# Layer 0's mixer reads x a second time in feature-major form, in place of transposing it on chip

## The chip, the cores and the metric

The kernel runs on one core of a Trainium2 chip. The metric is the device time in microseconds of one execution. The engines are TensorE (PE, with its weight loads as PEld), VectorE (DVE), ScalarE (ACT), GpSimd (POOL) and SyncE (SP), which issues the loads and stores. Each engine works through its own queue strictly in the order in which the program has it, and waits for the others by semaphores.

## The reference

Two residual layers over x of 1024 tokens by 1024 features in float32. Layer 0's mixer begins with an RMS norm and one input projection, whose columns go to a gated MLP (u, v) and to attention with eight heads (q, k, v):

```python
def rms_norm(x, g):
    xf = x.astype(jnp.float32)
    return xf * lax.rsqrt(jnp.mean(xf * xf, -1, keepdims=True) + EPS) * g.astype(jnp.float32)

def even_mixer(h, w_in, ...):
    z = h @ w_in
    u, v, q, k, vb = jnp.split(z, [...], axis=-1)
    ...
    qh = rms_norm(heads(q), q_g)
    kh = rms_norm(heads(k), k_g)
    vh = heads(vb).astype(jnp.float32)
    ...

for layer in range(DEPTH):
    h = rms_norm(x, norm_mix_g[layer]).astype(x.dtype)
    mix = even_mixer(...) if layer % 2 == 0 else gla_mixer(...)
    x = x + mix.astype(x.dtype)
    h = rms_norm(x, norm_ffn_g[layer]).astype(x.dtype)
    x = x + conv_ffn(h, ...)
```

The rest (attention with a band of 128 and two dilated branches, gated linear attention in layer 1, the convolutional MLPs) is not touched by the change.

## The kernel before

Every matrix product runs on operands split in two fp32r parts, a high part (a cast) and a remainder (source minus high part); `split` makes them, `PASSES` multiplies high by high, high by low and low by high. The norm of layer 0 is not applied to x: its gain g0 is folded into the weights (`load_qkv` with `scaled`), and the inverse root mean square of each token, `r0[:, n]`, is applied where a product is evacuated.

`even` prepares x. It loops over the eight token tiles n of 128 rows. Each is loaded as 128 tokens by 1024 features (three buffers, tag "x"), PE transposes its eight 128x128 blocks into PSUM (`pt`), and ACT and DVE split them into `hq`, the feature-major operand of the projections; `hq[g][h]` holds the features of parity g of tile half h. ACT then squares the tile with a running sum, and POOL makes `r0[:, n]` of it (`inv_rms`, two short operations). After tile 1 the weights of head pair 0 are loaded and split.

`attention` runs four head pairs. `project(p)` loops over the eight token tiles: 24 matmuls of 128x384 into an accumulator `pj` (two PSUM banks), and then, for each tile: ACT squares q and k (`qn`, needs r0), DVE sums, POOL makes the inverse norm (`rq`), DVE scales `qn` from the accumulator, and ACT evacuates v (`vN`). The accumulator is free for the tile after next when both have read it. POOL and DVE split q and k (`qs`, `ks`), PE transposes them (`tq`, `tk`), ACT casts `qT`, ACT or DVE `kT`. `unit` does one tile's banded attention: scores (`sc`), masked minimum on DVE and exponential on ACT (`sm`), transposes (`pP`), a copy (`pT`) and the product with v (`po`). `dilated(p)` and the projection of pair p + 1 follow.

The program text is not the final order: a scheduler with a cost model of its own reorders each engine's queue when the kernel is built. Loads go out on one SP queue with eight semaphores in rotation, so that each load's issue waits for the landing of the load eight places ahead of it.

## Time and profile before

| what | value |
|---|---|
| time, three runs | 2174.93, 2177.8 (median), 2179.95 us |
| profiled execution | 2178.69 us, span 2176.9 us |
| granted TensorE clock, mean | 0.998 |
| instructions | 29864 |
| PE, PEld busy | 98%, 83% |
| DVE, ACT, POOL busy | 70%, 48%, 23% |
| HBM read, written | 239.02 MB, 108.59 MB |

The span runs from the first to the last instruction of the profiled execution; what lies around it is 1.8 us. A row of the timeline gives the start, the duration, the engine, the line, the operation and its operands, and in brackets how long the engine had been idle before it and what ended that. A row by stretches gives the busy time of each engine with its number of instructions, the granted clock, the share of the DMA engines and the GB/s. A row by groups gives the count, the busy time, the mean of one in ns and the idle time before the group.

### The profile page before, as it was taken

Reading aid. Unit: us, or ns where it says so; the run is one execution under the profiler, and the core shown is the slowest. Engines: PE = TensorE matmul, PEld = TensorE weight load, DVE = VectorE, ACT = ScalarE, POOL = GpSimd, SP = SyncE. Lnnn points to the kernel's source line nnn. Section 1 sums busy time; section 2 is a strip of 40 time slices with the busy share of each in tenths; the row PEclk is TensorE's granted clock in tenths of the full one; section 3 lists DMA queues with packets and bytes.
Section 4 is the critical chain, followed back from the end, with each engine's and each line's share of the span. In section 5 each row is a group of like instructions: output and inputs, shape, how many; then the busy total and the mean of one; then the engine's idle time right before and its main releaser. Section 6 shows DMA issues by size and latency. Waiting matters only on the chain.

```text
span 2176.9 us, 29864 instructions
## 1 busy us (share of the span) xinstructions
PE 2139.8 (98%) x10508; PEld 1812.1 (83%) x10508; DVE 1534.4 (70%) x2451; ACT 1034.1 (48%) x1998; POOL 490.8 (23%) x519
## 2 busy tenths in 40 slices
PE   8999999999999999999999999999999999999999
PEld 7999988877888888878889888878788888888887
DVE  6566655567887988755576777667788878885554
ACT  6455545355444444444454455534544444444443
POOL 4444421013342434100020011100333424320000
PEclk9999999999999999999999999999999999999999
DMA  4122212655544444675564233386544444557555
GB/s 158 48 81 63 78 55 77 212 204 201 158 156 160 160 165 160 197 268 198 194 210 129 71 97 97 117 268 242 201 160 153 153 156 159 165 179 277 201 195 202
DMA packets 157254, 349.59 MB, mean 161 GB/s; under 512 B 17408, under 2 KB 54272, under 8 KB 156720
## 3 DMA queue, kind: packets, MB, share of 16 engines
q1 hardware_dynamic: 157104, 347.68, 47.6%
q8 instruction: 83, 1.36, 0.3%
q14 instruction: 67, 0.55, 0.1%
HBM read 239.02 MB, written 108.59 MB: 160 GB/s over the span
## 4 chain that ended last, share of the span: by engine, by line
PE 87%; DMA 5%; DVE 3%; ACT 3%; issue 1%; POOL 0%; SPq 0%; DVEq 0%; ACTq 0%; POOLq 0%
PE puB L290 11%; PE pgB L290 11%; PE pv L190 6%; PE pj L190 6%; PE pgC L290 5%; PE puC L290 5%; PE pdB L397 5%; PE pdC L397 5%; PE pdO L397 4%; PE po L190 3%; PE puA L290 3%; PE pgA L290 3%; PE pdQ L397 2%; PE pdP L397 2%; PE pu L190 2%; PE pBq L992 2%
## 5 line engine op out<-in xcount | busy, mean ns | idle before, releaser
L101 DVE TENSOR_TENSOR da<-ar,da 128x512 fp32r<-128x512 f32 x154 | 106.3, 690 | 157.3 <-ACT da L100 157.2
L100 ACT CAST da<-ar 128x512 fp32r<-128x512 f32 x154 | 95.9, 623 | 211.1 <-PE pdC L397 91.6
L190 PE MATMUL po<-wo,hq 128*128 128x512 f32 x768 | 184.4, 395 | 1.6 <-ACT hq L100 1.0
L190 PEld LDWEIGHTS po<-wo,hq 128*128 128x128 f32 x768 | 141.6, 188 | 31.7 <-ACT hq L100 1.4
L190 PE MATMUL pv<-wv,hq 128*128 128x512 f32 (+2 forms) x768 | 139.8, 339 | 2.1 <-DVE b L1024 1.6
L397 PE MATMUL pdB<-dw,da 128*128 128x512 f32 x528 | 136.2, 391 | 1.0 <-ACT dw L100 1.0
L397 PE MATMUL pdC<-dw,da 128*128 128x512 f32 x528 | 135.8, 390 | 0.0
L190 PEld LDWEIGHTS pv<-wv,hq 128*128 128x128 f32 x768 | 119.0, 189 | 17.4 <-DVE b L1024 2.1
L397 PEld LDWEIGHTS pdB<-dw,da 128*128 128x128 f32 x528 | 98.6, 188 | 22.3 <-ACT dw L100 1.4
L190 PE MATMUL pj<-wq,hq 128*128 128x384 f32 x576 | 116.2, 343 | 0.2 <-ACT vN L720 0.2
L397 PEld LDWEIGHTS pdC<-dw,da 128*128 128x128 f32 x528 | 99.1, 188 | 20.5
L256 POOL TENSOR_TENSOR S1g<-rg 128x512 f32<-128x512 f32 x20 | 29.4, 1470 | 382.6 <-DMA wsd<-D 235.0
L140 POOL TENSOR_SCALAR rn<-ssq 128x1 f32<-128x1 f32 x24 | 10.6, 441 | 465.0 <-ACT h L148 245.4
L101 DVE TENSOR_TENSOR dw<-wr,dw 128x512 fp32r<-128x512 f32 x154 | 105.8, 687 | 9.5 <-ACT dw L100 9.1
L397 PE MATMUL pdO<-dw,da 128*128 128x512 f32 x396 | 102.2, 389 | 0.2 <-DVE dw L101 0.2
L100 ACT CAST dw<-wr 128x512 fp32r<-128x512 f32 x154 | 95.0, 617 | 13.0 <-DMA wr<-in_w_dn 7.5
L190 PEld LDWEIGHTS pj<-wq,hq 128*128 128x128 f32 x576 | 99.2, 189 | 0.5 <-ACT vN L720 0.4
L397 PEld LDWEIGHTS pdO<-dw,da 128*128 128x128 f32 x396 | 74.2, 188 | 16.0 <-DVE dw L101 0.6
L319 DVE SCALAR_TENSOR_TENSOR t<-g,cw,t 128x1022 f32<-128x1022 f32 x44 | 75.6, 1719 | 0.1
L303 DVE TENSOR_TENSOR g<-g,s1g 128x512 f32<-128x512 f32 x22 | 17.2, 783 | 77.1 <-ACT s1g L302 77.0
L318 DVE SCALAR_TENSOR_TENSOR t<-g,cw,t 128x1023 f32<-128x1023 f32 x44 | 59.4, 1351 | 16.7 <-ACT t L317 16.7
L320 ACT ACTIVATE t<-t 128x1024 f32<-128x1024 f32 x44 | 46.7, 1061 | 30.7 <-DVE t L319 30.6
(1073 smaller groups left out, 5465.8 us busy)
## 6 DMA issues: line engine op xcount, KB each, us to landing
ar<-actd SPq DMA_DIRECT2D x70, 512.0 KB, 3.5
rd<-in_w_down SPq DMA_DIRECT2D x44, 512.0 KB, 3.7
wsd<-D SPq DMA_DIRECT2D x88, 256.0 KB, 2.5
rg<-in_w_gate SPq DMA_DIRECT2D x42, 512.0 KB, 3.6
ru<-in_w_up SPq DMA_DIRECT2D x42, 512.0 KB, 4.6
wr<-wsd SPq DMA_DIRECT2D x40, 512.0 KB, 4.2
actd<-t SPq DMA_DIRECT2D x66, 256.0 KB, 2.2
wr<-in_w_dn SPq DMA_DIRECT2D x30, 512.0 KB, 4.9
```

The lines of the kernel that those rows point to most:

```text
L100: (hi or A.copy)(dst[0], src)
L101: (lo or V.tensor_sub)(dst[1], src, f32(dst[0]))
L140: G.tensor_scalar(r, ssq, 1.0 / n, EPS, op0=ALU.mult, op1=ALU.add)
L190: T.matmul(o, L[i], R[jj][:, sl], start=(k == 0 and (ii, jj) == PASSES[0]), stop=(k == nk - 1 and (ii, jj) == PASSES[-1]))
L256: G.tensor_tensor(sums[name], x, y, op=op)
L290: T.matmul(o, L[ii][:, j * P : j * P + P], right[p][:, jj, j, :], skip_group_check=more, start=(not more and j == 0 and (ii, jj) == PASSES ...
L303: V.tensor_add(C22, C22, s1)
L318: V.scalar_tensor_tensor(t[:, 1:], g[:, : S - 1], w(1), t[:, 1:], op0=ALU.mult, op1=ALU.add)
L319: V.scalar_tensor_tensor(t[:, 2:], g[:, : S - 2], w(0), t[:, 2:], op0=ALU.mult, op1=ALU.add)
L320: A.activation(t, t, AF.Silu)
L397: T.matmul(o, L[ii][:, t * P : t * P + P], R[jj], skip_group_check=more, start=start and not more and (ii, jj) == PASSES[0], stop=stop and ...
L992: T.matmul(o, L[ii][:, j * P : j * P + P], right[p][:, jj, j, :], skip_group_check=more, start=(not more and j == 0 and (ii, jj) == PASSES ...
```

## The change

The host hands x over a second time as `x_T`: for each token tile the features on the partitions, ordered by parity g, by j and then by token (feature k * 128 + c with k = 2j + g), so that one tile is one 512 KB load and needs no transpose. ACT casts the high part of parity 0, POOL that of parity 1, DVE makes both remainders from SBUF. The token-major x is still loaded, for the squares alone, which are now made in place. The eight transposes per tile and their PSUM tiles are gone.

Every tile has a place: feature tiles 0 to 3 and token tiles 0 to 3 share six buffers, feature tiles 4 and 5 have two, feature tiles 6 and 7 stand in the room that `qR` of pair 1 takes later (`xq`), token tiles 4 to 7 in that of `kT` of pair 1 (`xk`). The squares of token tiles 4 to 7 are written inside the first projection, ahead of its tiles 0 to 3 (`rest`, called as `early`). The weights of pair 0 and the q and k gains are loaded after the first feature tile, ahead of all others; `gains` is the first five lines of `attention`, moved.

```diff
             with tc.tile_pool(name="nrm", bufs=1, reuse_waits="tile") as pool:
+                Q.dma_start(g0, a["norm_mix_gT"])
+                xk = pq.tile([P, 4, S], F32, tag="kT", bufs=1, name="xk")
+                xq = pq.tile([P, 2, S], F32, tag="qR", bufs=1, name="xq")
+
+                def home(name, tag, bufs):
+                    return pool.tile([P, D], F32, tag=tag, bufs=bufs, name=name)
+
+                def statistics(n, xt):
+                    ssq = small.tile([P, 1], F32, tag="ssq", name=f"ssq{n}")
+                    A.activation(xt, xt, AF.Square, accum_out=ssq)
+                    inv_rms(ssq, 1, D, f"rn{n}", r0[:, n : n + 1])
+
+                def token_rows(n):
+                    xt = home(f"x0{n}", "a", 6) if n < 4 else xk[:, n - 4]
+                    Q.dma_start(xt, rows(a["x"], n))
+                    if n < 4:
+                        statistics(n, xt)
+
                 for n in range(NT):
-                    xt = pool.tile([P, D], F32, tag="x", bufs=3, name=f"x0{n}")
-                    Q.dma_start(xt, rows(a["x"], n))
+                    xt = home(f"xf{n}", "a", 6) if n < 4 else home(f"xf{n}", "b", 2) if n < 6 else xq[:, n - 6]
+                    xf = xt.rearrange("p (g j t) -> p g j t", g=2, j=4)
+                    Q.dma_start(xf, a["x_T"][n])
+                    for g in range(2):
+                        split(place(hq[g][n // 4], n), xf[:, g], hi=G.tensor_copy if g else None)
                     if n == 0:
-                        Q.dma_start(g0, a["norm_mix_gT"])
-                    for g in range(2):
-                        pt = ps.tile([P, 4, P], F32, tag="pt", name=f"pt{n}{g}")
-                        for j in range(4):
-                            k = 2 * j + g
-                            T.transpose(pt[:, j, :], xt[:, k * P : (k + 1) * P], ident)
-                        split(place(hq[g][n // 4], n), pt)
-                    if n == 1:
                         wq0 = load_qkv(0, wx)
-                    h = pool.tile([P, D], F32, tag="h", bufs=2, name=f"h{n}")
-                    ssq = small.tile([P, 1], F32, tag="ssq", name=f"ssq{n}")
-                    A.activation(h, xt, AF.Square, accum_out=ssq)
-                    inv_rms(ssq, 1, D, f"rn{n}", r0[:, n : n + 1])
+                        gqk = gains(pq)
+                        token_rows(0)
+                    elif n > 1:
+                        token_rows(n - 1)
+                token_rows(NT - 1)
+
+            def rest(n):
+                if n < 4:
+                    statistics(n + 4, xk[:, n])
...
-        def project(p, ws=None, then=None):
+        def project(p, ws=None, then=None, early=None):
...
             for n in range(NT):
+                if early:
+                    early(n)
                 pj = ps.tile([P, 512], F32, tag="pj", name=f"pj{p}{n}")
...
-        made = project(0, wq0)
+        made = project(0, wq0, early=rest)
...
         "x": A["x"][0],
+        "x_T": A["x"][0].reshape(NT, P, 4, 2, P).transpose(0, 4, 3, 2, 1),
```

What this makes of the queues is seen at three places. The first is the SP queue before, from the third x tile on; `x` with its number is a token tile (tiles 2 to 4 here), `wq1` are weights of pair 1, `hg` and `gT` small tables of later stages.

```order
L523 DMA x_399<-in_x 128x1024
L647 DMA gqk<-in_q_g 128x64 [waits DMAHW0_49]
L648 DMA gqk<-in_k_g 128x64 [waits DMAHW1_49]
L523 DMA x_420<-in_x 128x1024 [waits DMAHW2_49,PE_49,Activation_49]
L647 DMA gqk<-in_q_g 128x64 [waits DMAHW3_49]
L648 DMA gqk<-in_k_g 128x64 [waits DMAHW4_49]
L1129 DMA hg<-in_head_g 128x2 [waits DMAHW5_49]
L460 DMA gT_5177<-in_norm_ffn_gT 128x8 [waits DMAHW6_49]
L110 DMA wq10r<-in_w_qkv 128x768 [waits DMAHW7_49,DVE_49]
L523 DMA x_441<-in_x 128x1024 [waits DMAHW0_49,PE_49]
L110 DMA wq11r<-in_w_qkv 128x768 [waits DMAHW1_49,DVE_49]
```

After, at the same depth of the queue (g0, feature tile 0, the four weight loads, four `gqk`, token tile 0 and feature tiles 1 and 2 stand ahead). `xf` and `xq` are feature tiles (3 to 7 here), `x_389`, `x_401` and `x_413` are token tiles 1, 2 and 3, `xk` token tiles 4 to 7.

```order
L535 DMA x_389<-in_x 128x1024 [waits DMAHW5_49]
L542 DMA xf_395<-in_x_T 128x1024 [waits DMAHW6_49]
L535 DMA x_401<-in_x 128x1024 [waits DMAHW7_49,DVE_49,Activation_49]
L542 DMA xf_407<-in_x_T 128x1024 [waits DMAHW0_49]
L542 DMA xf_419<-in_x_T 128x1024 [waits DMAHW1_49]
L535 DMA xk<-in_x 128x1024 [waits DMAHW2_49]
L542 DMA xq<-in_x_T 128x1024 [waits DMAHW3_49]
L535 DMA xk<-in_x 128x1024 [waits DMAHW4_49]
L542 DMA xq<-in_x_T 128x1024 [waits DMAHW5_49]
L535 DMA xk<-in_x 128x1024 [waits DMAHW6_49]
L535 DMA x_413<-in_x 128x1024 [waits DMAHW7_49,Activation_49]
L535 DMA xk<-in_x 128x1024 [waits DMAHW0_49]
```

All sixteen tiles of x now stand ahead of the weights of pair 1, and token tile 3 stands behind token tiles 4, 5 and 6.

The second place is ACT around the evacuations `vN` of tiles 0 and 1 (`vN_575` and `vN_651`) before; `x_441` to `x_483` are token tiles 4 to 6.

```order
L536 ACTIVATE h_457,ssq_458<-x_441 128x1024 [waits DMAHW0_49,Activation_49,Pool_49]
L712 ACTIVATE qn_566<-pj_541,r_84 128x256 [waits PE_49,Pool_49]
L105 ACTIVATE wq_0_1363<-wq11r,g_83 128x384 [waits DMAHW1_49]
L105 ACTIVATE wq_1_1366<-wq11r,g_83 128x384 [waits DVE_49]
L100 COPY hq_85<-pt_422 128x4x128 [waits PE_49]
L712 ACTIVATE qn_642<-pj_617,r_84 128x256 [waits PE_49,Pool_49]
L100 COPY hq_87<-pt_429 128x4x128 [waits PE_49]
L720 ACTIVATE vN_575<-pj_541,r_84 128x128 [waits DVE_49]
L536 ACTIVATE h_478,ssq_479<-x_462 128x1024 [waits DMAHW4_49,Activation_49]
L100 COPY hq_86<-pt_443 128x4x128 [waits PE_49]
L720 ACTIVATE vN_651<-pj_617,r_84 128x128 [waits DVE_49]
L536 ACTIVATE h_499,ssq_500<-x_483 128x1024 [waits DMAHW7_49,Activation_49,Pool_49]
```

After, from behind `vN` of tile 0 and the cast of feature tile 4 on: `vN_567` is that of tile 1, `x_413` is token tile 3, the three `xk` are token tiles 4 to 6, `hq_86` the casts of feature tiles 5 to 7.

```order
L737 ACTIVATE qn_558<-pj_533,r_84 128x256 [waits PE_49,Pool_49]
L100 COPY hq_86<-xf_419 128x4x128 [waits DMAHW1_49]
L100 COPY hq_86<-xq 128x4x128 [waits DMAHW3_49]
L758 COPY qT_499<-tq_496 128x256 [waits PE_49]
L737 ACTIVATE qn_640<-pj_615,r_84 128x256 [waits DVE_49,Pool_49]
L764 COPY kT_447<-tk_502 128x16x32 [waits PE_49]
L100 COPY hq_86<-xq 128x4x128 [waits DMAHW5_49]
L530 ACTIVATE x_413,ssq_415<-x_413 128x1024 [waits DMAHW7_49,Activation_49]
L530 ACTIVATE xk,ssq_449<-xk 128x1024 [waits DMAHW2_49]
L530 ACTIVATE xk,ssq_529<-xk 128x1024 [waits DMAHW4_49,Activation_49]
L530 ACTIVATE xk,ssq_611<-xk 128x1024 [waits DMAHW6_49,Activation_49]
L745 ACTIVATE vN_567<-pj_533,r_84 128x128 [waits DVE_49]
```

Before, one square stood between the two evacuations; after, the squares of four token tiles do, with `qT` and `kT` of tile 0 and the casts of four feature tiles.

The third place is PE ahead of the projection of tile 3 (`pj_773`) before; `pt` are transposes of x tiles 4 and 5.

```order
L190 MATMUL pj_695<-wq_1_383,hq_87 128x384 x3
L190 MATMUL pj_695<-wq_0_388,hq_85 128x384 x3
L530 MATMUL pt_450<-ident,x_441 128x128 [waits DVE_49]
L530 MATMUL pt_450<-ident,x_441 128x128 x3
L730 MATMUL tq_584<-identr,qs_578 128x128 [waits DVE_49]
L730 MATMUL tq_584<-identr,qs_578 128x128
L190 MATMUL pj_695<-wq_1_391,hq_87 128x384 x3
L530 MATMUL pt_464<-ident,x_462 128x128 [waits DMAHW4_49,DVE_49]
L530 MATMUL pt_464<-ident,x_462 128x128 x3
L190 MATMUL pj_773<-wx_364,hq_85 128x384 [waits Activation_49]
L190 MATMUL pj_773<-wx_364,hq_85 128x384 x2
```

After, the projection of tile 3 is `pj_697`, and `tq`, `tk` and `sc0n` are tile 0's.

```order
L190 MATMUL pj_615<-wq_0_359,hq_85 128x384 x3
L190 MATMUL pj_615<-wq_1_362,hq_87 128x384 x3
L755 MATMUL tq_496<-identr,qs_490 128x128 [waits DVE_49]
L755 MATMUL tq_496<-identr,qs_490 128x128
L763 MATMUL tk_502<-identr,ks_491 128x128 [waits Activation_49,Pool_49]
L763 MATMUL tk_502<-identr,ks_491 128x128 [waits DVE_49]
L763 MATMUL tk_502<-identr,ks_491 128x128 x2
L684 MATMUL sc0n_511<-kT_447,qT_499 128x128 [waits Activation_49]
L684 MATMUL sc0n_511<-kT_447,qT_499 128x128
L684 MATMUL sc0n_518<-kT_447,qT_499 128x128 x2
L190 MATMUL pj_697<-wx_335,hq_85 128x384 [waits Activation_49]
```

The transposes of x are gone from between the matmuls, and the transposes and scores of tile 0 now stand ahead of the projection of tile 3.

More of the change, by code (lines that the diff above doesn't have):

```diff
@@ L538, in even, with gains @@
+                token_rows(NT - 1)
+            def rest(n):
+                if n < 4:
+                    statistics(n + 4, xk[:, n])
             with tc.tile_pool(name="at", bufs=2, reuse_waits="tile") as at, \
                     tc.tile_pool(name="av", bufs=1, reuse_waits="tile") as av:
-                return attention(ps, at, av, pq, pq0, par0, wx, wq0, masks, gm_open)
+                return attention(ps, at, av, pq, pq0, par0, wx, wq0, gqk, masks, rest, gm_open)
+    def gains(pq):
+        gqk = pq.tile([P, 2, 2, 64], F32, name="gqk", bufs=1)
+        for s in range(2):
+            Q.dma_start(gqk[:, 0, s, :], a["q_g"].partition_broadcast(P))
+            Q.dma_start(gqk[:, 1, s, :], a["k_g"].partition_broadcast(P))
+        V.tensor_scalar(gqk[:, 0], gqk[:, 0], -0.125, None, op0=ALU.mult)
+        gqk = gqk.rearrange("p a s c -> p (a s c)")
+        return gqk
@@ L641, in u_proj, with attention @@
         proj512(ps, load_half(a["w_vu"][1], "wu", g0), "pu", consume)
-    def attention(ps, at, av, pq, pq0, par0, wx, wq0, masks, gm_open):
-        gqk = pq.tile([P, 2, 2, 64], F32, name="gqk", bufs=1)
-        for s in range(2):
-            Q.dma_start(gqk[:, 0, s, :], a["q_g"].partition_broadcast(P))
-            Q.dma_start(gqk[:, 1, s, :], a["k_g"].partition_broadcast(P))
-        V.tensor_scalar(gqk[:, 0], gqk[:, 0], -0.125, None, op0=ALU.mult)
-        gqk = gqk.rearrange("p a s c -> p (a s c)")
+    def attention(ps, at, av, pq, pq0, par0, wx, wq0, gqk, masks, rest, gm_open):
         mband, mboth = masks
```

## The prediction

> **What bounds the kernel now.** I read the page first, then busy time by stretches of the start, then the engines' timeline there.

> ```profile
> PE 2139.8 (98%) x10508; PEld 1812.1 (83%) x10508; DVE 1534.4 (70%) x2451; ACT 1034.1 (48%) x1998; POOL 490.8 (23%) x519
> PE   8999999999999999999999999999999999999999
> ```

> TensorE (PE) is busy for 2139.8 of 2176.9 us, and only the first fortieth of the span, 54.4 us, shows less than nine tenths. The change touches just that fortieth. Behind it, what arrives late there stays late, so I ask at what time the PE queue reaches the same point of its program before and after. Busy time by stretch:

> ```profile
> core 0: us, PE busy (x) PEld busy (x) DVE busy (x) ACT busy (x) POOL busy (x), PEclk, DMA share, GB/s
> 0.00:10.00 10.00, 4.49 (x18) 3.65 (x19) 6.23 (x17) 6.59 (x12) 3.06 (x13) 1.00 0.82 277
> 10.00:20.00 10.00, 10.00 (x52) 9.93 (x52) 5.96 (x12) 7.28 (x16) 1.49 (x4) 1.00 0.74 272
> 20.00:30.00 10.00, 6.60 (x31) 6.29 (x30) 6.46 (x14) 7.15 (x16) 7.43 (x15) 0.70 0.67 240
> 30.00:40.00 10.00, 10.00 (x66) 9.86 (x65) 4.05 (x9) 5.08 (x11) 4.79 (x10) 0.96 0.19 61
> 40.00:50.00 10.00, 8.46 (x63) 7.75 (x62) 7.64 (x22) 5.58 (x16) 5.61 (x10) 1.00 0.01 2
> 50.00:60.00 10.00, 9.86 (x73) 9.43 (x72) 3.89 (x12) 4.67 (x14) 2.13 (x5) 1.00 0.13 37
> ```

> PE loses 5.5 us in the first stretch, 3.4 in the third and 1.5 in the fifth. In the third the granted clock falls to 0.70 on average. The timeline and two short stretches show how:

> ```profile
> 21.15 0.60 PE L530 MATMUL pt<-ident,x 128*128 128x128 f32 x4
> 25.15 1.12 PE L530 MATMUL pt<-ident,x 128*128 128x128 f32 x4 [3.40 <-DVE hq L101]
> 25.92 4.19 PE L190 MATMUL pj<-wx,hq 128*128 128x384 f32 x12
> 128.73 4.24 PE L190 MATMUL pj<-wq,hq 128*128 128x384 f32 x23
> 23.00:24.00 1.00, 0.00 (x0) 0.00 (x0) 0.10 (x1) 0.76 (x2) 0.98 (x1) 0.96 0.63 247
> 30.00:31.00 1.00, 1.00 (x6) 1.00 (x5) 0.00 (x1) 0.00 (x0) 0.14 (x1) 0.62 0.00 0
> ```

> PE stops at 21.75. The clock halves at about 23.9 (0.96 over that microsecond) and is whole again at about 30.8 (0.62), 5.6 us after work resumed. In between a 128x384 matmul takes 0.335 to 0.35 us; at full clock it takes 0.18 (23 in 4.24). This price returns below.

> **The change part by part. What it removes.** The 64 transposes of x go, with what PE waited for them:

> ```profile
> L530 PE MATMUL pt<-ident,x 128*128 128x128 f32 x64 | 11.9, 322 | 8.7 <-DMA x<-in_x 4.7 <-DVE hq L101 4.0
> L100 ACT CAST hq<-pt 128x512 fp32r<-128x512 f32 x16 | 9.3, 582 | 7.2 <-PE pt L530 7.1
> L101 DVE TENSOR_TENSOR hq<-pt,hq 128x512 fp32r<-128x512 f32 x16 | 11.0, 685 | 11.4 <-ACT hq L100 11.4
> L100 POOL CAST ks<-qn 128x256 fp32r<-128x256 f32 x13 | 5.6, 429 | 0.3 <-PE tk L738 0.3
> ```

> PE is relieved of 11.9 us of busy time. ScalarE (ACT) keeps 8 of its 16 casts, so it gives up 4.7 us. GpSimd (POOL) takes the other 8; no row has its 128x512 cast, but at twice the 0.43 us of the 128x256 one it is at most 0.86, about 7 us in all, on an engine that is busy for 12 of the first 30 us. VectorE (DVE) does the same 16 subtractions, now from SBUF. If PE were what sets the end of this stage, some 10 us would be won.

> **What it adds: eight more loads of 512 KB ahead of everything else.** What a load costs in the queue:

> ```profile
> 0.79 0.39 SPq L523 DMA_DIRECT2D x<-in_x  x1
> 4.61 1.06 ACT L536 ACTIVATE h<-x 128x1024 f32<-128x1024 f32 x1 [2.55 <-DMA x<-in_x]
> 7.83 0.33 SPq L647 DMA_DIRECT2D gqk<-in_q_g  x1
> 8.79 0.33 SPq L648 DMA_DIRECT2D gqk<-in_k_g  x1
> 9.76 0.33 SPq L1129 DMA_DIRECT2D hg<-in_head_g  x1
> 10.74 0.33 SPq L460 DMA_DIRECT2D gT<-in_norm_ffn_gT  x1
> 12.07 0.33 SPq L110 DMA_DIRECT2D wq10r<-in_w_qkv  x1
> 14.85 1.06 ACT L536 ACTIVATE h<-x 128x1024 f32<-128x1024 f32 x1 [0.78 <-DMA x<-in_x]
> ```

> From the ninth load on, each issue waits for the load eight places ahead of it. So 7.83, 8.79, 9.76 and 10.74 are the landings of the four 384 KB weight loads of pair 0, and 12.07 is that of x tile 2. That is 0.97 us per 384 KB and 1.3 per 512 KB. The next 512 KB tile landed at 14.85, 2.8 us later, with two of the small broadcast loads of gqk between: 0.73 us for each of those.

> In the changed SP order I add these up. The gain vector g0 goes first, so the feature-major tile 0 lands at 4.61 + 0.44 = 5.05. The weights follow with one tile less ahead of them, 7.83 - 1.3 = 6.5, 7.5, 8.5 and 9.4. Four gqk loads at 0.73 make 12.3. Then come fourteen 512 KB tiles up to and including token tile 3, which stands behind token tiles 4, 5 and 6: 12.3 + 14 x 1.31 = 30.6. Before, the same token tile landed at 14.85. With eight loads in flight the issue itself never runs dry. The gqk price could be nothing if small loads overlap; then token tile 3 lands at 27.7.

> **The wait that this makes.** The ACT queue is in program order, and in it the evacuation of v of tile 1 (vN, "vN1") now stands behind the square of token tile 3 and those of tiles 4, 5 and 6. The projection's accumulator has two banks, so projection tile 3 ("pj3") cannot start before vN1. Prices:

> ```profile
> L536 ACT ACTIVATE h<-x 128x1024 f32<-128x1024 f32 x8 | 8.4, 1055 | 5.2 <-DMA x<-in_x 5.2
> L536 ACT ACTIVATION_READ_ACCUMULATOR h<-x 128x1 f32 x8 | 1.5, 189 | 0.0
> 28.38 0.37 ACT L720 ACTIVATE vN<-pj,r 128x128 f32<-128x128 f32 x1 [1.49 <-DVE qn L716]
> 33.38 2.33 PE L190 MATMUL pj<-wx,hq 128*128 128x384 f32 x12
> 46.30 0.33 PE L730 MATMUL tq<-identr,qs 128*128 128x128 f32 x2 [0.85 <-DVE kT L739]
> 53.32 2.31 PE L190 MATMUL pj<-wx,hq 128*128 128x384 f32 x12
> 70.33 0.50 PE L738 MATMUL tk<-identr,ks 128*128 128x128 f32 x4 [0.62 <-ACT qT L733]
> 71.74 1.10 PE L689 MATMUL po0n<-vN,pT0n 128*128 128x64 f32 x8 [0.91 <-DVE pT0n L686]
> ```

> A square with its read takes 1.15 us pitch (1.055 + 0.189, overlapping by 0.1). So vN1 ends at 30.6 + 4 x 1.15 + 0.37 = 35.6, and pj3 starts there. Before, it started at 33.38.

> Is anything else later than that? Tile 0's projection ends at about 13.5, because its last weight lands at 9.4 and DVE needs 0.6 us for each of eight weight remainders from 6.9 on, with 0.65 lost to the wait for gqk. Tile 1's features land at 14.9; its second half waits for DVE until about 18, and it ends at 21.6 (24 if the clock has halved in between). Tile 2 then waits for v of tile 0, at about 21.6, behind the square of token tile 2 that lands at 20.1; it ends at 26 to 28. Nothing more for PE to do but tq, tk and the two scores of tile 0, until about 28.5. So PE idles some 7 us before pj3, and the transposes that were removed would have fitted in there. The other steps on ACT ahead of token tile 3's square (qT and kT of tile 0, the cast of feature tile 7) end at about 28.6. This is the floor if the loads come early: pj3 at 28.6 + 4.6 + 0.37 = 33.6.

> From pj3 to the start of pj5 it took 19.94 us before (33.38 to 53.32). After, in the changed PE order:
> - pj3 with two small transposes. An idle time of 7 us is over the 2.2 after which the clock halved, so I take half clock for 5.6 us: 15.4 matmuls and the transposes, then 8.6 x 0.18 = 1.55. Together 7.15. At full clock throughout it would be 4.6; for 7 us of half clock, 0.65 more.
> - tq of tile 1: 0.25. pj4 with tk of tile 1 and po of tile 0: 24 x 0.18 + 0.7 = 5.0.
> - the units of tiles 1 to 3 up to pj5. Before, they took 46.30 to 53.32, 7.0 us; pP0 and po0, now done earlier, and tq4, now done inside pj5, make 1.4 less: 5.6. ACT casts and scores follow one another there with little cover, so I take 6.3, half way. PE's own work in it, some 4.6, is the lower end; 8.5 (pj4's end at 44.8 to 53.32) the upper.

> pj5 starts at 35.6 + 7.15 + 0.25 + 5.0 + 6.3 = 54.3, 1.0 us later than before. Later, at the end of the first projection, five weight splits instead of seven stand ahead of qT of tile 5 on ACT, and two waits of PE (0.62 and 0.91) shrink. Between nothing and 1.1 us is won; I take 0.5. Sum: 1.0 - 0.5 = 0.5 us slower. The profiled execution took 2178.69 us, 0.9 above the median of 2177.8; on the median the forecast is 2178.3.

> [...]

> **The rivals.**
> 1. Forecast: the load of token tile 3 and four squares hold pj3, and the time stays within 0.2% (4.4 us, about what a measurement of this kernel can tell from no change). For it: in-order ACT and two banks leave no way round, and floor and sum for pj3 lie at 33.6 and 35.6, on both sides of 33.38. Chance 0.63. Its own range, from all bounds: 0.5 - 2.0 - 2.5 - 1.7 - 0.6 = -6.3 to 0.5 + 0.65 + 2.2 + 0.5 = +3.9, not all ends at once.
> 2. Faster: the loads land at their floor, the clock stays whole through the gap because small steps keep PE awake, and the units run at PE's pace: 2178.3 - 2.0 - 2.5 - 1.7 = 2172.1, or 2171.5 with all of the later win. Against it: it takes all three at once, and the 7 us hole has no matmul in it. Chance 0.15.
> 3. Slower: the load queue. 14 tiles at 1.31 us assume 400 GB/s without a hole, but the stretches above show means of 240 to 277. If a tile takes 1.6 us, token tile 3 lands 4.1 us later; from 1.6 us on this alone decides. At 1.75 (300 GB/s) pj3 starts 6.2 us later, at 41.8, and the time is 2184.5. For it: the queue was never this full for this long before. Against: whenever it was full, it ran at 0.97 us per 384 KB. Chance 0.22, with what else can hold PE at half clock through tiles 1 and 2.

> **The numbers.** Rivals 2 and 3 stand on either side, and I let the range reach into both: 2173.0 to 2185.0. Faster by more than 0.2% 0.15, within 0.63, slower 0.22.

> **What would show it.** In the changed profile: no L530 transposes; token tile 3's square at 30 to 31 us, three more squares behind it, then vN; PE idle for 5 to 8 us before pj3, released by ACT vN; the granted clock at 0.5 after that; pj3 at 33.5 to 36 and pj5 at 52 to 56. I am wrong if vN1 is done by 30, if the loads have landed by 26 or only after 34, or if PE shows no hole there.

## The result and the profile after

The changed kernel takes 2179.67 us (median of 20 runs, 2177.46 to 2182.53) where the kernel before takes 2176.14 us (20 runs, 2172.61 to 2179.95). The ratio is 1.0014, 95% interval 1.0007 to 1.002: slower by about a seventh of a percent, inside the 0.2% that the prediction called no change. The profiled execution took 2179.2 us, its span 2177.5.

The page of the changed kernel, PE's busy time and its slices:

```profile
PE 2135.6 (98%) x10444; PEld 1808.7 (83%) x10444; DVE 1534.2 (70%) x2451; ACT 1032.2 (47%) x1990; POOL 497.8 (23%) x527
PE   7999999999999999999999999999999999999999
```

The 64 transposes are gone, but PE's busy time fell by only 4.2 us, not by their 11.9, mostly because other matmuls ran at half clock for longer (15.3 us of busy time at half clock against 5.6, the stretches below); and the first slice shows a tenth less work. The start by stretches, with the columns of the table in the prediction:

```profile
0.00:10.00 10.00, 3.36 (x9) 2.69 (x10) 7.50 (x20) 5.62 (x10) 2.16 (x10) 1.00 0.64 218
10.00:20.00 10.00, 7.82 (x32) 6.60 (x31) 6.36 (x12) 5.96 (x11) 4.98 (x9) 0.93 0.97 390
20.00:30.00 10.00, 8.19 (x45) 7.76 (x43) 6.53 (x12) 5.15 (x12) 7.79 (x14) 0.90 1.03 409
30.00:40.00 10.00, 6.01 (x22) 5.98 (x23) 6.38 (x16) 8.03 (x20) 9.28 (x19) 0.66 0.65 211
40.00:50.00 10.00, 8.85 (x60) 7.96 (x60) 4.89 (x14) 3.69 (x11) 5.38 (x11) 1.00 0.12 41
```

The loads run at 390 to 409 GB/s from 10 to 30 us (272 and 240 before), and PE's longest wait has moved to the fourth stretch. The timeline there, ACT first and then PE:

```profile
29.42 1.06 ACT L530 ACTIVATE x<-x 128x1024 f32<-128x1024 f32 x1 [0.20 <-DMA x<-in_x]
32.56 1.04 ACT L530 ACTIVATE xk<-xk 128x1024 f32<-128x1024 f32 x1
33.60 0.35 ACT L745 ACTIVATE vN<-pj,r 128x128 f32<-128x128 f32 x1
28.75 0.66 PE L684 MATMUL sc0n<-kT,qT 128*128 128x128 f32 x4 [0.68 <-ACT kT L764]
33.99 4.21 PE L190 MATMUL pj<-wx,hq 128*128 128x384 f32 x12 [4.58 <-ACT vN L745]
40.94 2.32 PE L190 MATMUL pj<-wx,hq 128*128 128x384 f32 x12
52.61 2.33 PE L190 MATMUL pj<-wx,hq 128*128 128x384 f32 x12
```

This is the wait that the prediction described: the square of token tile 3 when its load lands, the squares of tiles 4, 5 and 6 behind it, then vN of tile 1, and pj3 behind that after 4.58 us without work. But pj5 starts at 52.61 us, 0.7 us earlier than in this profile of before (53.32). What is lost is lost later, and for another reason. The same table in stretches of 3.41 us, at places where the granted clock (third number from the right) changes; first the kernel before, then the changed one:

```profile
20.51:23.92 3.41, 1.24 (x11) 0.97 (x8) 1.87 (x4) 3.25 (x8) 2.52 (x4) 1.00 0.84 319
23.92:27.34 3.42, 2.19 (x8) 2.19 (x9) 2.62 (x6) 1.99 (x4) 2.45 (x7) 0.50 0.87 298
27.34:30.75 3.41, 3.41 (x12) 3.41 (x12) 1.45 (x4) 1.41 (x3) 2.59 (x6) 0.50 0.08 21
30.75:34.16 3.41, 3.41 (x24) 3.34 (x24) 1.04 (x2) 1.66 (x4) 0.73 (x2) 1.00 0.16 29
68.30:71.71 3.41, 1.91 (x15) 1.47 (x13) 3.41 (x7) 2.76 (x7) 2.51 (x4) 1.00 0.64 177
```

```profile
18.59:22.00 3.41, 3.41 (x12) 3.41 (x11) 2.46 (x4) 1.91 (x4) 3.27 (x6) 0.50 1.03 412
28.83:32.24 3.41, 0.59 (x4) 0.45 (x4) 3.01 (x10) 3.21 (x6) 3.25 (x5) 1.00 1.03 403
32.24:35.65 3.41, 1.66 (x5) 1.66 (x6) 0.70 (x2) 3.41 (x12) 2.94 (x9) 0.50 0.65 217
35.65:39.07 3.42, 3.42 (x12) 3.42 (x12) 3.42 (x8) 2.38 (x6) 3.42 (x6) 0.50 0.35 88
69.79:73.20 3.41, 2.09 (x15) 1.95 (x16) 3.41 (x8) 1.16 (x3) 1.24 (x4) 1.00 0.68 159
73.20:76.61 3.41, 3.41 (x13) 3.41 (x12) 2.33 (x8) 1.14 (x4) 2.53 (x4) 0.50 0.71 227
144.88:148.29 3.41, 2.10 (x14) 1.38 (x13) 2.42 (x8) 2.25 (x6) 2.97 (x6) 1.00 0.38 139
148.29:151.71 3.42, 3.42 (x17) 3.42 (x17) 1.40 (x6) 1.72 (x6) 1.47 (x3) 0.50 0.07 19
```

At these places the clock is 1.00 or 0.50 for a whole number of such stretches, each 3.41 us long; I call one at half clock a half stretch. Before has two, near 24 to 31 us. After has five: three at the start, one at 73 us and one at 148 us, where the projection of one pair runs into the rest of the pair ahead of it. A half stretch full of work costs an estimated 1.7 us, half its length: the 12 matmuls of pj3 took 4.21 us in two of them, 12 of the same shape 2.32 us at 40.94 us, behind them. The first 12 to 14 us of both kernels must be added: the column shows 1.00 there, but the matmuls take nearly twice the time that they take behind it, as these rows of the changed kernel show (in before four transposes take 1.12 us at 7.21 us and 0.60 at 15.13):

```profile
6.64 4.71 PE L190 MATMUL pj<-wx,hq 128*128 128x384 f32 x12 [6.64 <-ACT wx L105]
11.15 2.56 PE L190 MATMUL pj<-wq,hq 128*128 128x384 f32 x12
```

The granted clocks given here leave this start out. PE works through the same program, so the offset can be read off any tile: when the last u projection ends, the changed kernel is 1.9 us late (387.94 against 386.04 us). From there on PE has the same order in both, and that rest, to the last matmul, took 1783 to 1790 us in the thirteen profiles of this study, whichever the kernel.

### The profile page after: what moved, and what is told of

The parts are those of the page before. It is cut to its first block, busy times and chain, and to the rows that moved or that the text cites. A ratio compares the mean times of both kernels' runs of the same rounds, so it can differ in the third digit from the quotient of the medians.

```text
span 2177.5 us, 29722 instructions
## 1 busy us (share of the span) xinstructions
PE 2135.6 (98%) x10444; PEld 1808.7 (83%) x10444; DVE 1534.2 (70%) x2451; ACT 1032.2 (47%) x1990; POOL 497.8 (23%) x527
## 4 chain that ended last, share of the span: by engine, by line
PE 87%; DMA 5%; DVE 4%; ACT 3%; issue 1%; POOL 1%; SPq 0%; DVEq 0%; ACTq 0%
PE puB L290 11%; PE pgB L290 11%; PE pv L190 6%; PE po L190 6%; PE pgC L290 5%; PE puC L290 5%; PE pdB L397 5%; PE pdC L397 5%; PE pj L190 4%; PE pdO L397 4%; PE puA L290 3%; PE pgA L290 2%; PE pdQ L397 2%; PE pdP L397 2%; PE pu L190 2%; PE pBq L1017 2%
## 5 line engine op out<-in xcount | busy, mean ns | idle before, releaser
L101 DVE TENSOR_TENSOR da<-ar,da 128x512 fp32r<-128x512 f32 x154 | 106.2, 689 | 158.1 <-ACT da L100 158.0
L100 ACT CAST da<-ar 128x512 fp32r<-128x512 f32 x154 | 95.9, 623 | 210.7 <-PE pdC L397 90.5
L190 PE MATMUL po<-wo,hq 128*128 128x512 f32 x768 | 183.8, 394 | 1.3 <-ACT hq L100 1.0
L190 PEld LDWEIGHTS po<-wo,hq 128*128 128x128 f32 x768 | 141.7, 188 | 30.7 <-ACT hq L100 1.4
L190 PE MATMUL pv<-wv,hq 128*128 128x512 f32 (+2 forms) x768 | 139.8, 339 | 2.1 <-DVE b L1049 1.6
L190 PEld LDWEIGHTS pv<-wv,hq 128*128 128x128 f32 x768 | 119.0, 189 | 17.5 <-DVE b L1049 2.1
L190 PE MATMUL pj<-wq,hq 128*128 128x384 f32 x576 | 118.4, 350 | 0.0
L101 DVE TENSOR_TENSOR dw<-wr,dw 128x512 fp32r<-128x512 f32 x154 | 105.6, 686 | 8.4 <-ACT dw L100 8.0
L190 PEld LDWEIGHTS pj<-wq,hq 128*128 128x128 f32 x576 | 102.4, 195 | 0.1
L100 ACT CAST dw<-wr 128x512 fp32r<-128x512 f32 x154 | 95.0, 617 | 13.1 <-DMA wr<-in_w_dn 7.4
```

The source lines that it names most:

```text
L100: (hi or A.copy)(dst[0], src)
L101: (lo or V.tensor_sub)(dst[1], src, f32(dst[0]))
L190: T.matmul(o, L[i], R[jj][:, sl], start=(k == 0 and (ii, jj) == PASSES[0]), stop=(k == nk - 1 and (ii, jj) == PASSES[-1]))
```

## The experiments

The theory with which I went on: the changed start gains, and more half stretches of the clock eat the gain. The rival: the loss is the wait for loads and squares itself. In the table, "clock" is the mean granted clock over all runs of the kernel (0.001 is 2.2 us of the span), and "u ends" the time in its profile at which the last u projection ends; the ratio of after is that of the first 20 runs.

| kernel | ratio to before, 95% | clock | u ends, us |
|---|---|---|---|
| before (87 runs; two profiles) | 1 | 0.9983 | 386.04, 389.23 |
| after (31 runs; two profiles) | 1.0014 (1.0007 to 1.002) | 0.9954 | 387.94, 388.13 |
| e2_late | 1.0025 (1.0014 to 1.0037) | 0.9945 | 393.27 |
| e3_home | 0.9983 (0.9974 to 0.9992) | 0.9977 | 380.89 |
| e4_both | 0.9999 (0.999 to 1.0008) | 0.9964 | 385.39 |
| e5_filled | 1.0008 (0.9998 to 1.0017) | 0.9968 | 389.00 |
| e6_home_filled | 0.998 (0.997 to 0.999) | 0.9981 | 381.71 |
| e7_home_gains_later | 0.9994 (0.9985 to 1.0003) | 0.9968 | 382.24 |
| e9_fill70 | 1.0014 (1.0005 to 1.0023) | 0.9956 | 387.65 |
| e10_fill_both | 0.9995 (0.9985 to 1.0005) | 0.9978 | 384.78 |
| e11_home_scalar | 0.997 (0.996 to 0.9981) | 0.9986 | 380.25 |

**The changed kernel and the kernel before once more.**

> The changed kernel once more, for a second profile of the same instructions. Theory: its extra time over the kernel before comes from the order of the instructions at the two places where one pair's projection meets the next, where TensorE stands still once for about 1.6 us instead of twice for under 1 us and the clock then falls to half. If so the granted clock is again near 0.5 to 0.6 at 73 to 77 us and at 148 to 152 us, projection tile 3 again starts near 34 us, tile 5 near 52.6 us, and the time is 2179 to 2181 us. Rival: the two slow stretches were chance of one execution; then the clock reads 1.00 there and the second profile ends about 3 us earlier.

> The kernel before once more, for a second profile of the same instructions. Theory: the places of the half clock move with a grid of 3.41 us whose phase is another one in each execution, so that the one stretch near 24 to 31 us may start elsewhere within 3.4 us, and the holes near 69 to 73 us and 143 to 147 us may drop the clock here though they didn't in the first profile; from 390 us to the end it takes 1783 to 1785 us (1786.7 us in the first profile, whose time was 2.5 us above the median). Rival: the changed kernel's own last 1785 us are longer for a reason of their own; then before shows clearly less than 1783 us there.

The changed kernel: 2180.05 us, ratio 1.0015 (1.0007 to 1.0024). Its second profile halves the clock at 73.6 and 148.7 us again, 0.4 us later than the first, and starts pj5 at 52.92 us (52.61). So far the theory. But the kernel before, in its second profile (2183.33 us, slower than any of the 29 runs beside it), does it too:

```profile
18.35:21.76 3.41, 1.38 (x10) 0.82 (x8) 1.97 (x4) 3.25 (x7) 0.44 (x2) 1.00 0.91 354
21.76:25.17 3.41, 0.00 (x0) 0.00 (x0) 2.41 (x6) 2.63 (x7) 2.59 (x4) 0.50 0.64 205
69.55:72.96 3.41, 2.27 (x16) 1.99 (x17) 3.41 (x8) 1.03 (x3) 2.29 (x5) 1.00 0.74 192
72.96:76.37 3.41, 3.41 (x13) 3.41 (x12) 1.74 (x5) 0.00 (x0) 1.80 (x4) 0.50 0.60 180
148.06:151.47 3.41, 3.41 (x20) 3.41 (x19) 1.90 (x6) 2.12 (x7) 2.27 (x4) 0.50 0.00 0
151.47:154.88 3.41, 3.41 (x14) 3.41 (x13) 1.82 (x4) 0.00 (x0) 0.50 (x2) 0.50 0.29 85
```

Its waits there are the ones of the first profile (0.63, 0.91 and 0.23 us); only the stretches lie some 2.1 us differently against the program (the wait of 0.91 us ends 1.3 us into one here, 3.4 us into one there). It starts pj5 at 52.34 us, so at pj5 the two kernels can't be told apart. So a half stretch at 73 us is no mark of the change. What the change alters is how often it comes, and that only many runs show: the mean granted clock of the changed kernel is 0.995 or 0.996 in all 31 runs, that of the kernel before 0.998 or more in 73 of 87. Within the 87 runs of before, the time follows the clock: 2173.84 us on average at 1.000 (11 runs), 2177.7 at 0.998 (34), 2180.8 at 0.996 (6), a slope of 1.8 us for 0.001. By that slope the clock alone costs the changed kernel an estimated 5.3 us more than before (0.0029), over the 3.5 us by which it is slower. At an equal clock it would be faster by an estimated 1 to 2 us: runs at 0.996 took 2180.8 us before (6 runs) and 2179.1 after (12), runs at 0.995 2181.3 (2) and 2180.6 (19). The profiles agree: with five half stretches ahead of 390 us the last u projection ends at 389.23 us in before and at 387.94 and 388.13 in the changed kernel. For the rest from there on, before showed 1786.7 and 1788.2 us, not the 1783 to 1785 that I had expected of it, and the changed kernel 1785.3 and 1783.3, so the rival of this run falls.

**Squares later.** The squares of token tiles 4 to 7 are written two tiles later and pinned.

```diff
-                    A.activation(xt, xt, AF.Square, accum_out=ssq)
+                    sq = A.activation(xt, xt, AF.Square, accum_out=ssq)
+                    if n > 3:
+                        tc.keep_in_program_order(sq)
...
-                if n < 4:
-                    statistics(n + 4, xk[:, n])
+                if 2 <= n < 6:
+                    statistics(n + 2, xk[:, n - 2])
```

> The squares of token tiles 4 to 7 are issued two tiles later inside the first projection and held there, so that the copy vN of tile 1 stands behind the square of token tile 3 alone instead of behind four squares. Theory: the start gives back three squares of 1.04 us: projection tile 3 starts near 31 us instead of 34 us and the whole is 2 to 3.5 us shorter, 2176 to 2178 us, if the two later places stay as they are. Rival: tile 3 is held by something else (the scores of tile 0, the load of the features), or what is gained is lost again before tile 5; then tile 5 still starts near 52.6 us and the time stays at 2179.7 us.

A miss for both: slower, 2184.53 us in the median. The profile is of the slowest of the 11 runs (2189.01 us at a clock of 0.991). In it vN of tile 1 does follow the square of token tile 3 (30.60 to 31.66 us) and starts at 32.45 us, but now it waits 0.71 us for DVE, the start having run at half clock from 17.04 to 23.87 us; pj3 starts at 32.88, 1.1 us earlier. Then the shorter waits between the tiles' units fall into one stretch, and the clock stays low for three:

```profile
44.35:47.76 3.41, 2.00 (x14) 1.53 (x14) 2.34 (x7) 1.80 (x6) 1.03 (x2) 1.00 0.00 0
47.76:51.18 3.42, 3.42 (x19) 3.20 (x17) 1.19 (x4) 3.31 (x10) 1.34 (x3) 0.50 0.01 2
51.18:54.59 3.41, 3.41 (x18) 3.10 (x18) 2.62 (x7) 1.99 (x7) 0.76 (x3) 0.50 0.07 19
54.59:58.00 3.41, 3.41 (x13) 3.41 (x13) 0.73 (x3) 0.92 (x4) 2.28 (x5) 0.50 0.27 82
```

With two more near 75 us and one at 153 us, the edit that shortens the wait loses 5.3 us by 390 us in this profile. The scheduler also moved other instructions behind it, so this shows that the clock can undo a shorter wait, not that later squares are bad.

**Token tile 3 loaded early.** Token tiles 2 and 3 get the buffers of feature tiles 4 and 5 and the other way round, so that the load of token tile 3 waits for no square and stands six loads earlier.

```diff
-                    xt = home(f"x0{n}", "a", 6) if n < 4 else xk[:, n - 4]
+                    xt = home(f"x0{n}", *(("a", 6) if n < 2 else ("b", 2))) if n < 4 else xk[:, n - 4]
...
-                    xt = home(f"xf{n}", "a", 6) if n < 4 else home(f"xf{n}", "b", 2) if n < 6 else xq[:, n - 6]
+                    xt = home(f"xf{n}", "a", 6) if n < 6 else xq[:, n - 6]
```

> Token tiles 2 and 3 get the two buffers that feature tiles 4 and 5 had and these take used ones, so that the load of token tile 3 waits for no square and stands six loads earlier in SP's queue; the four squares still stand ahead of vN of tile 1. Theory: token tile 3 lands near 22 us instead of 29.4 us, vN of tile 1 then waits for the squares of the tiles that land up to about 28 us, projection tile 3 starts near 30 us instead of 34 us, and the time is 2175 to 2177 us. Rival (load queue): the last squared tile lands as late as before, since the bytes ahead of it are the same, and nothing changes: tile 3 at 33 to 34 us, 2179 to 2180 us.

> Both edits: token tile 3 loaded early, and the squares of token tiles 4 to 7 later. Theory: vN of tile 1 waits for no load and no square, so projection tile 3 follows the scores of tile 0 near 28.5 to 29 us without a hole of over 1 us, the clock doesn't fall to half there, and the whole is 5 to 6.5 us shorter than the changed kernel, 2173 to 2175 us, which would be below the kernel before too (2176.1 us). Rival: the gain stops at tile 5, whose features now land last (near 29 us), or the loss of the changed kernel lies later; then 2177 to 2180 us.

The exchange alone makes the kernel faster than both: 2173.34 us, ratio 0.9983 (0.9974 to 0.9992). Its squares and the tile behind them:

```profile
23.04 1.05 ACT L530 ACTIVATE x<-x 128x1024 f32<-128x1024 f32 x1
27.96 0.59 ACT L764 CAST kT<-tk 128x512 fp32r<-128x512 f32 x1 [0.31 <-PE tk L763]
28.44 1.06 ACT L530 ACTIVATE xk<-xk 128x1024 f32<-128x1024 f32 x1
30.00 1.06 ACT L530 ACTIVATE xk<-xk 128x1024 f32<-128x1024 f32 x1
31.58 0.37 ACT L745 ACTIVATE vN<-pj,r 128x128 f32<-128x128 f32 x1 [0.42 <-DVE qn L741]
32.00 3.85 PE L190 MATMUL pj<-wx,hq 128*128 128x384 f32 x12 [2.73 <-ACT vN L745]
```

pj3 starts 2.0 us earlier, not 4: two squares still stand between the cast kT of tile 0 and vN, which then waits 0.42 us for DVE. The profile has two half stretches in all of the first 390 us (18 and 32 us) and none at 70 or 145 us, and the last u projection ends 7.0 us earlier than in the changed kernel. Its clock rose from 0.9954 to 0.9977; by the slope an estimated 4 of the 6 us or more that were gained are the clock's, and the rest is left for the shorter wait. With the later squares added (e4_both, 2174.82 us) two half stretches stand at 69.6 to 76.4 us; the gain over before is gone (0.9999). pj3 starts at 30.79 us there, held by a vN that waits 1.35 us for DVE, not at 28.5 to 29. The time lies in the range that I expected, but before took 2175.47 us beside it: that both edits together would be clearly below before was wrong.

**Work put into the holes.** This is the test of the clock by itself: matmuls whose output is overwritten, placed where PE waits, with every other instruction of every engine in its old place.

```diff
             pts = ps.tile([P, 2, nj, P], F32, tag="pt", name="pP" + name)
+            if name == "0n0":
+                for i_ in range(18):
+                    d = T.matmul(pts[:, 0, 0, :], ident, mband[:, :P], start=True, stop=True)
+                    if i_ == 0:
+                        tc.keep_in_program_order(d)
```

> The changed kernel with 18 matmuls of 128x128 added, whose output is overwritten, behind the transposes of tile 0's keys, where TensorE stands still until projection tile 3; no other instruction of any engine changes its place. [...] At about 0.15 us each they fill 2.7 us or more of the 5.3 us without work, so one stretch at half clock less: tile 3 still starts near 34 us, the tiles behind it take 2.2 us each and not 3 to 4 us, and everything behind is 0.8 to 2.5 us earlier, 2177 to 2179 us. Rival: the clock only follows from what the loads allow, or added work on a TensorE that is busy for 98% of the span costs its own 2.7 us; then the time is the same or up to 2.7 us longer.

> The same 18 added matmuls in the kernel of the exchanged buffers (e3_home), again with no other instruction moved. There the hole ahead of tile 3 is about 4 us with two short pieces of work in it. Theory: the stretch at half clock behind it (3.41 us) goes, everything behind is 1.7 us earlier, 2171 to 2172.5 us by the whole against 2173.3 us. Rival: no gain, 2173 to 2176 us.

> The changed kernel with 6 added matmuls of 128x128 (some 0.24 us each, output overwritten) in the hole of 1.55 us near 70 us alone, behind the transposes of a key tile and ahead of the products that wait for VectorE's copy pT; no other instruction of any engine changes its place. Theory: nothing but the clock is touched, and the stretch of 3.41 us at half clock that followed this hole in both profiles of the changed kernel (near 73 to 77 us) is gone; everything behind 77 us is 1.7 us earlier, the mean granted clock of the runs goes from 0.9954 to about 0.9962, and the ratio to before falls from 1.0014 to about 1.0006. Rival: 1.4 us of added work delay what is behind them, or the clock falls anyway, since the small products around the hole don't count as enough work; ratio 1.0014 to 1.002.

> The changed kernel with both fillings, the 18 matmuls ahead of projection tile 3 (e5_filled) and the 6 near 70 us; again no other instruction changes its place. Theory: the gains add up, 1.4 us (e5_filled by the ratios) and 1.7 us: ratio about 0.9998 to 1.0002, so with 24 matmuls more the changed kernel comes level with the kernel before. Rival: a stretch saved in one place comes back in another, since the grid of 3.41 us is only met by other holes; ratio 1.0008 or more.

e9_fill70 has 6 of them under `"0n5"` alone, e10_fill_both 18 and 6; each shows as two records, so that x12 stands for 6. The 18 took 4.25 us in the hole. In e5_filled one half stretch (34.4 to 37.8 us, behind a stretch that was busy for 1.68 of 3.41 us) is left where there were two, as expected, though how much work a stretch needs for the clock to stay whole is not shown; the clock rises from 0.9954 to 0.9968 and the ratio falls to 1.0008, though its interval overlaps that of the changed kernel. (This profile, 2183.08 us, is one of the slowest of the 12 runs, 2178.03 in the median, and has three more half stretches, at 72 us and from 147 to 154 us.) Near 70 us (e9_fill70) the 6 do locally what was expected:

```profile
69.59 1.57 PE L700 MATMUL pP0n<-mband,ident 128*128 128x128 f32 x12
71.34 1.10 PE L716 MATMUL po0n<-vN,pT0n 128*128 128x64 f32 x8 [0.18 <-DVE pT0n L713]
73.05 3.98 PE L190 MATMUL pj<-wq,hq 128*128 128x384 f32 x22
```

The same place in the changed kernel:

```profile
71.09 1.10 PE L712 MATMUL po0n<-vN,pT0n 128*128 128x64 f32 x8 [1.55 <-DVE pT0n L709]
72.79 5.58 PE L190 MATMUL pj<-wq,hq 128*128 128x384 f32 x22
```

The wait of 1.55 us is down to 0.18 and the 22 matmuls behind it take 3.98 us in place of 5.58. Yet the whole gained nothing (1.0014, clock 0.9956): two half stretches stood at 145 to 152 us in this profile in place of one. The rival of this run, that the time isn't won, holds for the whole. Both fillings together (e10_fill_both) gave 0.9995 (0.9985 to 1.0005) at a clock of 0.9978, a little better than the theory's 0.9998 to 1.0002, which the interval covers: with 24 useless matmuls more, the changed kernel is level with before, and the interval doesn't reach that of the changed kernel. The two places where the work was added, in its profile:

```profile
34.62 2.35 PE L190 MATMUL pj<-wx,hq 128*128 128x384 f32 x12 [1.44 <-ACT vN L749]
71.20 3.99 PE L190 MATMUL pj<-wq,hq 128*128 128x384 f32 x22
```

The 12 matmuls of pj3 took 4.21 us in the changed kernel, the 22 took 5.58. With two half stretches ahead of 390 us, as in the first profile of before, the last u projection ends at 384.78 us against 386.04. Since nothing else was moved, this places the loss in the clock. Why the two together gain more (0.0019 of the ratio) than each alone (0.0006 and nothing) is not shown; the intervals of about 0.001 to either side leave room for chance.

On the exchanged buffers, e6_home_filled keeps the clock whole through the start, but its gain over e3_home (0.998 against 0.9983) can't be told from none; the tile behind pj3 now waits for its own vN:

```profile
31.30 2.34 PE L190 MATMUL pj<-wx,hq 128*128 128x384 f32 x12
37.45 2.35 PE L190 MATMUL pj<-wx,hq 128*128 128x384 f32 x12 [1.71 <-ACT vN L750]
```

**Two parts of the start.** The first, on top of e3_home, puts the gains behind feature tile 1; the second, on top of e6_home_filled, gives the high parts of feature tiles 0 and 1 back to ScalarE.

```diff
-                        gqk = gains(pq)
                         token_rows(0)
                     elif n > 1:
                         token_rows(n - 1)
+                    if n == 1:
+                        gqk = gains(pq)
```

> The kernel of e3_home with the four small loads of the gains put behind the load of feature tile 1. Theory of the prediction: each of the four costs the queue about 0.73 us, so feature tile 1 and the token tile ahead of it land about 2.2 to 2.9 us earlier (tile 1 near 11.5 us, not 14 us), projection tile 1 starts near 12.5 us, not 14.5 us, but the tiles behind the small loads land as late as before, so pj2 and tile 3 gain nothing: 2172 to 2174 us. Rival: the gain passes through to tile 3, and the time is 2170.5 to 2171.5 us.

```diff
-                        split(place(hq[g][n // 4], n), xf[:, g], hi=G.tensor_copy if g else None)
+                        split(place(hq[g][n // 4], n), xf[:, g], hi=G.tensor_copy if g and n > 1 else None)
```

> The kernel of e6_home_filled with one part of the change undone for feature tiles 0 and 1: the high parts of the odd half come from ScalarE again and not from GpSimd. Theory: projection tile 1 waits twice at 13.5 to 18 us, the second time 1.09 us for a remainder that VectorE makes behind GpSimd's high part; ScalarE needs 0.6 us for such a part, so this wait shrinks to 0.5 us or less and the later tiles keep their time from the loads: ratio 0.9975 to 0.998. Rival: ScalarE's longer list delays the square of token tile 0 and the first normalisation, and tile 3 with them; ratio 0.9985 or more.

With the gains later, pj1 starts at 13.31 us (14.54 in e3_home) and then stands still for 2.80 us until 16.62; vN of tile 1 starts at 31.47 us against 31.58. Nothing passes through, as expected; the time, 2175.4 us, lies above the 2172 to 2174 us expected, and the ratio 0.9994 is no better than that of e3_home. The price of a small load could not be read from the time.

With ScalarE's casts the second wait of pj1 is gone, and pj2 starts at 19.39 us, 2.1 us earlier than in e6_home_filled; pj3 at 29.55, 1.75 earlier:

```profile
14.64 2.81 PE L190 MATMUL pj<-wx,hq 128*128 128x384 f32 x12 [0.94 <-ACT hq L100]
19.39 2.35 PE L190 MATMUL pj<-wx,hq 128*128 128x384 f32 x12
29.55 2.38 PE L190 MATMUL pj<-wx,hq 128*128 128x384 f32 x12
```

2171.33 us, ratio 0.997 (0.996 to 0.9981), the fastest version here, and its profile has no half stretch before 2168 us. Against e6_home_filled the intervals overlap; and of the 1.75 us at pj3, 1.5 are left at 390 us, about what one half stretch at 142.6 us cost e6_home_filled. How much of it is ScalarE's stays open.

## Why the prediction held, and where it did not

The forecast was 2178.3 us, no change within 0.2%, with 2173.0 to 2185.0 as the range; the median is 2179.67. No change within 0.2% is what came, but not by the terms of the sum: by the medians the change costs 3.5 us where 0.5 was forecast. That this still lies within the 4.4 us of "no change" is in part luck, since two errors of opposite sign partly cancel, in the first pair of profiles 1.7 us too much up to pj5 and 3.1 us too little behind it.

- **The wait.** Right in its mechanism, link by link, and 1.6 us too long. Token tile 3's square started at 29.42 us (30.6 forecast). SP's issue at 12.71 us waits for the load eight places ahead, so token tile 0 had landed then, where the sum has 13.6 us: the four gqk loads cost an estimated 0.5 us each (from the last weight's landing at 9.39 us, and 1.28 for the tile), not 0.73. The 13 tiles behind it took 1.28 us each, not 1.31. The square itself started only 0.2 us after ACT was free, so load and list of ACT held it about equally. Squares follow one another every 1.04 us, not 1.15. So vN1 ended at 33.95 (35.6) and pj3 started at 33.99 (35.6). PE was idle for 4.58 us just before it, 5.3 with the 0.68 ahead of the scores, not 7 (in the second profile 6.15 and 6.8).
- **The half clock behind it.** From pj3's start to pj4's it took 6.95 us; 7.15 and 0.25 were forecast. The size was right, taking the 5.6 us for a length of its own was not: the half clock in before lasts two stretches, 6.83 us from 23.92 us on, and PE was busy for only 2.19 of the 3.42 us of the first. Behind that one the clock stayed at half, behind the second, busy for all of its 3.41 us, it was whole again; the 5.6 us are what was left of the two when work resumed at 25.15 us.
- **pj4 and the units.** 5.07 us (5.0) and 6.6 (6.3).
- **pj5.** 52.61 and 52.92 us in the two profiles, where 54.3 was forecast; before has 53.32 and 52.34, so the start is neutral, not 1.0 us later. The ten microseconds of transposes did go into the wait, as the prediction had it.
- **Later: -0.5 us.** This is the step of the sum that failed, in size and sign. I looked at two waits of PE at 70 to 72 us and counted their length. The changed order makes of them one wait of 1.55 us behind DVE, and what follows costs more than either: half clock at 73 us and again at 148 us, +2.6 us from pj5 to 390 us in the first pair of profiles. The terms held nothing on the clock behind the start, because the one profile of before that I had shows it whole there; the second one doesn't.
- **Rivals.** The slower one (the load queue at 300 GB/s) is refuted: 390 to 409 GB/s. The faster one needed three things at once: the clock whole through the gap (it halved; e10_fill_both shows what a whole one is worth), the loads at their floor (29.42 us, not 27.7) and the units at PE's pace (6.6 us, not 4.6).

## What to carry to other kernels

On a kernel that PE bounds, count a wait twice: its length, and the half clock that may follow it, which came in stretches of 3.41 us here, each worth up to an estimated 1.7 us more (half its length). One profile shows one position of these stretches against the program, so compare the mean granted clock of many runs before saying that a place is free of it. Where a wait can't be removed, work put into it for nothing can pay, though not in each place by itself: 24 useless matmuls in two waits brought the changed kernel level with the one before, 6 in one of them gained nothing.

## What the runs showed of the hardware

PE's busy time in a stretch alone doesn't decide which clock follows. 1.91 of 3.41 us kept the clock (before, at 68.30 us) and 2.27 of 3.41 lost it (its second profile, at 69.55 us); it was kept with as little as 1.61 us (the changed kernel, at 1448.78 us) and lost with as much as 2.32 (the second profile of before, at 144.65 us). So no one share of a stretch divides the two. The way back is no different: 2.19 us (before, at 23.92) and 3.12 (e9_fill70, at 144.80) didn't bring the full clock and 3.31 (e3_home, at 31.89) did, but 2.84 us of 128x384 products alone were enough in e5_filled (in the stretch that ends at 20.75 us: 7 products took 2.61 us from 17.91 us on, 12 took 2.24 from 22.61), and three stretches that were busy from end to end were not: at 148.06 us in the second profile of before and at 47.76 and 51.18 us in e2_late, all three shown above. The stretch that lost the clock with 2.27 us held the 128x64 products with v (1.10 us), the one that kept it with 1.91 didn't reach them. Whether the size of the products decides it was not shown.
